# Delayed low halves, an earlier fourth split and later last-head products in a two-layer SSD and attention kernel

## The chip, the cores and the metric

The kernel runs on one core of a Trainium2 chip. The metric is the device time of one execution in microseconds, shown as the median of several runs of the same program. The engines are TensorE (PE in the profile, its weight load PEld), VectorE (DVE), ScalarE (ACT), GpSimd (POOL) and SyncE (SP), which here only starts transfers. POOL starts transfers too.

## The reference

A model of two layers at 512 positions and width 1024, in float32. Layer 0 is a state-space mixer, layer 1 is latent attention with 16 heads. Cut to the second layer, where the change lies:

```python
proj = u @ in_w
c_q, c_kv, k_r, z = split(proj)                      # 384, 256, 64, 2048 columns
q  = (rms_norm(c_q) @ uq_w)                          # 16 heads of 128 + 64 (rotated)
kv = (rms_norm(c_kv) @ ukv_w)                        # 16 heads of 128 (k) + 128 (v)
s = concat(q_nope, rope(q_rope)) @ concat(k_nope, rope(k_r)).T * scale
p = softmax(where(key <= query, s, -inf))            # causal, blocks of 128 queries
o = (p @ v).reshape(512, 2048) * silu(z)
h = h + o @ out_w
return rms_norm(h, final_norm_w)
```

## The kernel before

Every large product is made three times over in a reduced float format (fp32r): each operand is split into a high part, a cast by ACT, and a low part, the rest, a subtraction on DVE; PE then adds high x high, high x low and low x high. So each operand that reaches PE brings a cast and a subtraction, and PE has three matmuls of 128x128 by 512 where one would do.

*Weights* (`weight`, `prefetch`, `load_weight`, `split_weight`). A weight tile is 128 x 1024 (512 KB), or 128 x 640 or 128 x 512. Asking for weight i starts the load of weight i+3 from POOL's queue into one of two `raw` buffers (L303), casts weight i+2 on ACT into `whi` (L312), and puts its subtraction `wlo` (DVE, L63 of the helper) on a list. A load into a raw buffer waits until the subtraction that read the buffer is done.

*Attention.* From about 440 us the order of PE's instructions is written out by hand, and in the head loop SP, DVE, ACT and POOL also work in the written order. For head h the loop has a `feed`: the projections for later heads (`front_a`, `front_b`, `front_v` for q, k and v of a pair of heads, `zgemm` for the gate), and from head 11 on chunks of the output projection (L1061), 4, 4, 4, 8 and 10 of them. The feed yields after every six matmuls, called a tick. Between ticks stand the `pieces`, each at a share of the loop's cost:

- at SC: the four blocks of scores of head h+1 (L871, L874, L876) and then its fetch;
- at TU: `turn(h, kb)`, which splits the fetched block kb of head h: cast `ph` on ACT (L932), subtraction `pl` on DVE (L933);
- at PR: `product(h, kb)`, three matmuls with v (`po`, L947);
- at ZS = 0.8, after heads 3, 7 and 11: four silus of gates on ACT, with a change of its function table.

A score block goes through a masked minimum on DVE (L881, L883), exp on ACT (L257), a reciprocal on DVE (L889), a scaling by it (blocks 2 and 3 on ACT, L891; blocks 0 and 1 on DVE, L893) and a transpose of 32x32 tiles on DVE (`pb`, L900). Four transfers per block write it to memory (`pd<-pb`, L904), and `fetch` reads it back turned (`pl<-pd`, L925), in four transfers. Scores of a head are made one loop before its splits and products.

`defer(fn, lag)` puts an instruction off by that many ticks (`tick`), or until somebody who needs it calls `now()`. The rope of a pair's q (three DVE operations on `rraw` and `rsw`, L742 to L744) is put off by three ticks, other subtractions by one. In the output projection `out_tok` adds a chunk's result to the residual (`hr`, L1065), and `cut` makes its operands, `ah` on ACT and `al` on DVE. The output projection is made in two halves of eight heads each.

Of the kernel before, what the change touches and what calls it, by code (L numbers as in the profile page):

```python
# [10 lines left out]
F32 = mybir.dt.float32  # L11
F32R = mybir.dt.float32r
AF = mybir.ActivationFunctionType
ALU = mybir.AluOpType

P = 128
T = 512
# [6 lines left out]
MH = 16  # L24
# [17 lines left out]
G7 = 33.0  # L42
SF = (0.6, 1.0, 2.0, 3.2, 8.0)
SC = (0.0, 0.06, 0.14, 0.22, 0.6)
TU = (0.18, 0.25, 0.46, 0.57)
PR = (0.35, 0.45, 0.74, 0.94)
ZS = 0.8
KO = (4, 4, 4, 8, 10)
MID = 4
# [113 lines left out]
class Net:  # L163
# [142 lines left out]
    def split_weight(self, raw, cuts=()):  # L306
        nc = self.nc
        n = raw.shape[1]
        hi = self.whi.tile([P, n], F32R, tag="hi", name=self.nm("whi"))
        lo = self.wlo.tile([P, n], F32R, tag="lo", name=self.nm("wlo"))  # L310
        for a, b in zip((0, *cuts), (*cuts, n)):
            nc.scalar.copy(hi[:, a:b], raw[:, a:b])  # L312
            self.wlater.append(self.defer(functools.partial(
                nc.vector.tensor_tensor, lo[:, a:b], raw[:, a:b], hi[:, a:b].bitcast(F32), op=ALU.subtract)))
            yield
        yield hi, lo

# [373 lines left out]
    def mla(self):  # L691
        tc, nc, t, wk = self.tc, self.nc, self.t, self.wk
# [10 lines left out]
        for k in range(KD):  # L703
            h = self.h[k]
            a = self.act.tile([P, T], F32R, tag="ah", name=self.nm("vh"))
            b = self.act.tile([P, T], F32R, tag="al", name=self.nm("vl"))
# [6 lines left out]
        for i in range(6):  # L713
# [15 lines left out]
            while pend and i >= NU:  # L729
                o = self.o16.tile([P, T], F32, tag="o", name=self.nm("cq"))  # L730
# [16 lines left out]
        lo, hi = slice(0, 64), slice(64, 128)  # L747
# [8 lines left out]
        def zgemm(i):  # L756
            w = self.weight("w", U_MZ + i)
            ps = self.bank("mm")
            yield from self.gemm(ps[:], w, vh, vl, KD)
            z = self.o16.tile([P, T], F32, tag="o", name=self.nm("z"))  # L760
            v.tensor_tensor(z[:], ps[:], r1[:], op=ALU.mult)
            zt.append(z)
            yield 8 * 0.216
# [57 lines left out]
        def front_b(j):  # L821
            f = F[j]
            w = self.weight("ub", j)
            ps = self.bank("mm")
            yield from self.gemm(ps[:], w, qh, ql, 3)
            f["q", 1], e = qsplit(ps[:])
            f["w"].append(e)
            yield 0.2
            ps = self.bank("mm")
            yield from self.gemm(ps[:], w, kh, kl, 2, 384)  # L830
            f["k", 1], e = ksplit(ps[:])
            f["w"].append(e)
            yield 1.3

        def front_v(j):
            f = F[j]
            wh, wl = self.weight("uc", j)
            f["v"] = []
            for half in range(2):
                ps = self.bank("mm")  # L840
                for c2 in range(2):
                    c = 2 * half + c2
                    s = slice(c * P, (c + 1) * P)
                    seq = []
                    for k in range(2):
                        wc = slice(k * 256, k * 256 + 256)
                        seq += [(kh[k][:, s], wh[:, wc]), (kh[k][:, s], wl[:, wc]), (kl[k][:, s], wh[:, wc])]
                    for i, (a, b) in enumerate(seq):
                        nc.tensor.matmul(ps[:, c2 * 256:(c2 + 1) * 256], a, b, start=i == 0, stop=i == 5)
                va = wk.tile([P, T], F32R, tag="va", name=self.nm("va"), bufs=3)  # L850
                vb = wk.tile([P, T], F32R, tag="vb", name=self.nm("vb"), bufs=3)
                nc.scalar.copy(va[:], ps[:])
                f["w"].append(self.defer(functools.partial(
                    v.tensor_tensor, vb[:], ps[:], va[:].bitcast(F32), op=ALU.subtract)))
                f["v"].append((va, vb))
                yield 1.3
# [94 lines left out]
        def chain(*gs):  # L951
            for g in gs:
                yield from g
# [21 lines left out]
        def steps(h):  # L975
            return [functools.partial(score, h, b) for b in range(NCH)] + [functools.partial(fetch, h)]
# [10 lines left out]
        lo, hi = slice(0, 64), slice(64, 128)  # L987
# [11 lines left out]
        with self.tc.manual_schedule(engines={E.SP, E.DVE, E.Activation, E.Pool}):  # L999
            self.lagging, self.look = True, 2  # L1000
            self.sched(chain(front_b(0), front_v(0), zgemm(4)), list(zip(SF, steps(0))))
            for h in range(MH):
                feed, cost = [], 0.0
                j = h // 2 + 1
                if h < 14:
                    feed.append(front_a(j) if h % 2 == 0 else front_b(j))
                    cost += 5.2 if h % 2 == 0 else 5.9
                if h < 11:
                    feed.append(zgemm(5 + h))
                    cost += 5.2  # L1010
                if h >= 11:
                    k = KO[h - 11]
                    feed.append(itertools.islice(outg, k))
                    cost += 1.3 * k
                if h % 2 and h < 14:
                    feed.append(front_v(j))
                at = SC if h + 1 < MH else ()
                pieces = [(x * cost, fn) for x, fn in zip(at, steps(h + 1))]
                pieces += [(x * cost, functools.partial(turn, h, b)) for b, x in enumerate(TU)]
                pieces += [(x * cost, functools.partial(product, h, b)) for b, x in enumerate(PR)]  # L1020
                if h < 13 and h % 4 == 3:
                    pieces.append((ZS * cost, functools.partial(zsilu, h // 4 + 1)))
                if h == 10:
                    pieces.append((0.8 * cost, functools.partial(self.cut, zt, 0, 4)))
                self.sched(chain(*feed), pieces)
            self.run(outg)
            self.run(self.out_tok(zt, 1, None))

    def cut(self, o, half, n):
        done = self.cuts.setdefault(half, [])  # L1030
        while len(done) < min(n, 8):
            src = o[8 * half + len(done)][:]
            a = self.act.tile([P, T], F32R, tag="ah", name=self.nm("ah"))
            b = self.act.tile([P, T], F32R, tag="al", name=self.nm("al"))
            self.nc.scalar.copy(a[:], src)
            done.append((a, b, self.defer(functools.partial(
                self.nc.vector.tensor_tensor, b[:], src, a[:].bitcast(F32), op=ALU.subtract))))

    def out_tok(self, o, half, hd):
        nc, wk, v, t = self.nc, self.wk, self.nc.vector, self.t  # L1040
# [50 lines left out]
        for n in range(2):  # L1091
            last = half == 1 and n == 1
            cuts = [(c, 0, T) for c in range(NCH)]
            if last:
                cuts[-1:] = [(NCH - 1, 0, T // 2), (NCH - 1, T // 2, T)]
            ps = [self.bank("ot") for _ in cuts]
            base = U_OUT1 + 8 * half + 4 * n
            for u in range(2 if last else 4):
                w = self.weight("w", base + u)
                self.cut(o, half, 2 * u + 2 + OA)  # L1100
                fresh = half == 0 and u == (0 if n else 2)
                if fresh:
                    for _, _, e in hl:
                        e.now()
                for q, (c, a, b) in zip(ps, cuts):
                    if fresh:
                        r = self.o16.tile([P, T], F32, tag="o", name=self.nm("hr"))
                        nc.sync.dma_start(r[:], hd[c, :, n * T:(n + 1) * T])
                        if n == 0:
                            self.hh.append([])  # L1110
                        self.hh[c].append(r)
                    step(q, c, w, n, (2 * u, 2 * u + 1), u == 0, u == 3, a, b)
                    if b == T:
                        yield 1.3
                    if u == 3:
                        done(q, c, n)
                if half == 0 and n == 1:
                    self.cut(o, 1, 2 * u + 2)
            if last:
                w2, w3 = self.weight("w", base + 2), self.weight("w", base + 3)  # L1120
                for q, (c, a, b) in zip(ps, cuts):
                    step(q, c, w2, n, (4, 5), False, False, a, b)
                    step(q, c, w3, n, (6, 7), False, True, a, b)
                    done(q, c, n, a, b)
                    yield 2.6
# [77 lines left out]
```

## Time and profile before

| | |
|---|---|
| median of 3 runs | 855.61 us (854.59 to 856.98) |
| the profiled execution | 854.5 us |
| its span in the trace | 852.5 us |
| mean granted clock of PE | 0.991 |
| busy, share of the span | PE 96%, PEld 80%, DVE 77%, ACT 55%, POOL 6% |
| matmul records | 4068 |

Starts in the trace are counted from the span's start. The profiled execution lies 1.1 us under the median, so a time worked out in the trace is compared with 854.5 first, and then set against the median. In a row of the timeline the first two numbers are the start and the duration in us; a bracket at its end tells how long the engine had been idle and on what it waited. In a row of waits the numbers after the colon are the total, the count and the longest. `x2` at the end means two neighbours of one kind in one row.

### The profile page before, as it was taken

The numbers are of one execution on the slowest core, as the hardware profiler recorded it, in microseconds if no ns is written. First come the engines' busy times: TensorE is split into PE (matmuls) and PEld (weight loads), VectorE is DVE, ScalarE is ACT, GpSimd is POOL, SyncE is SP. The second block draws the span as 40 slices with busy tenths as digits, with TensorE's granted clock in tenths as the row PEclk, the third lists the DMA queues.
The fourth block names the chain that finished last, engine by engine and source line by source line (L and its number), as shares of the span: only waits on it lengthen the run. The fifth ranks groups of instructions, "written<-read, shape, count | busy, mean of one in ns | idle before, by whom it ended". The sixth has DMA issues, their size and how long they took to land.

```text
span 852.5 us, 11895 instructions
## 1 busy us (share of the span) xinstructions
PE 815.8 (96%) x4068; PEld 678.7 (80%) x4068; DVE 660.1 (77%) x1266; ACT 468.6 (55%) x826; POOL 50.9 (6%) x100
## 2 busy tenths in 40 slices
PE   7999999999999999999999999999999997997995
PEld 5887888888888888888888787887877876876885
DVE  6999898879888889776674978687786886865444
ACT  7566764656564648252443655556567556653233
POOL 0000000000000000000011120111101110100000
PEclk9999999999999999999999999999999999999998
DMA  7364543424242423425453256665655655576312
GB/s 224 103 193 130 168 154 99 140 84 148 92 156 75 149 88 111 136 74 148 113 139 110 64 134 160 137 142 137 158 145 138 146 156 129 138 185 175 97 63 99
DMA packets 144492, 111.57 MB, mean 131 GB/s; under 512 B 108592, under 2 KB 116272, under 8 KB 144432
## 3 DMA queue, kind: packets, MB, share of 16 engines
q1 hardware_dynamic: 134944, 79.61, 34.0%
q0 software_dynamic: 8768, 30.15, 11.7%
q10 hardware_dynamic: 720, 1.05, 0.3%
q8 instruction: 32, 0.52, 0.3%
q14 instruction: 28, 0.23, 0.1%
HBM read 93.60 MB, written 14.81 MB: 127 GB/s over the span
## 4 chain that ended last, share of the span: by engine, by line
PE 62%; DVE 13%; DMA 10%; ACT 7%; issue 4%; SPq 4%; DVEq 0%; POOL 0%; ACTq 0%
PE mm L332 40%; PE ot L1061 7%; DMA pd<-pb 4%; PE mm L341 4%; DMA pl<-pd 3%; SPq L904 3%; PE yd L149 2%; DVE wlo L63 2%; PE s L871 2%; ACT whi L312 2%; PE yd L332 1%; PE aux L141 1%; DVE pl L933 1%; PE po L947 1%; PE aux L116 1%
## 5 line engine op out<-in xcount | busy, mean ns | idle before, releaser
L312 ACT CAST whi<-raw 128x1024 fp32r<-128x1024 f32 (+3 forms) x132 | 127.0, 966 | 184.0 <-PE mm L332 162.3
L63 DVE TENSOR_TENSOR wlo<-raw,whi 128x1024 fp32r<-128x1024 f32 (+3 forms) x132 | 146.6, 1115 | 45.5 <-ACT whi L312 45.0
L332 PE MATMUL mm<-ah,whi 128*128 128x512 f32 x384 | 153.9, 401 | 0.0
L332 PE MATMUL mm<-ah,wlo 128*128 128x512 f32 x384 | 150.1, 391 | 0.4 <-DVE wlo L63 0.4
L332 PE MATMUL mm<-al,whi 128*128 128x512 f32 x384 | 149.8, 390 | 0.0
L332 PE MATMUL mm<-vh,wlo 128*128 128x512 f32 x224 | 87.7, 392 | 1.2 <-DVE wlo L63 1.2
L332 PE MATMUL mm<-vh,whi 128*128 128x512 f32 x224 | 88.3, 394 | 0.2 <-ACT whi L312 0.2
L332 PE MATMUL mm<-vl,whi 128*128 128x512 f32 x224 | 87.3, 390 | 0.0
L332 PEld LDWEIGHTS mm<-ah,wlo 128*128 128x128 f32 x384 | 72.1, 188 | 16.1 <-DVE wlo L63 0.8
L332 PEld LDWEIGHTS mm<-ah,whi 128*128 128x128 f32 x384 | 72.2, 188 | 15.4 <-issue 1.4
L332 PEld LDWEIGHTS mm<-al,whi 128*128 128x128 f32 x384 | 72.2, 188 | 14.4 <-DVE al L353 0.3
L303 POOL DMA_DIRECT2D raw<-in_w_dram x36 | 19.3, 537 | 602.4 <-DMA hd<-ht 417.0
L933 DVE TENSOR_TENSOR pl<-pl,ph 128x512 fp32r<-128x512 f32 (+1 forms) x64 | 30.8, 482 | 31.2 <-ACT ph L932 31.2
L1061 PE MATMUL ot<-whi,ah 128*128 128x512 f32 (+1 forms) x136 | 52.1, 383 | 0.0
L1061 PE MATMUL ot<-wlo,ah 128*128 128x512 f32 (+1 forms) x136 | 51.8, 381 | 0.0
L1061 PE MATMUL ot<-whi,al 128*128 128x512 f32 (+1 forms) x136 | 51.8, 381 | 0.0
L332 PEld LDWEIGHTS mm<-vh,wlo 128*128 128x128 f32 x224 | 42.0, 188 | 11.4 <-DVE wlo L63 2.1
L332 PEld LDWEIGHTS mm<-vh,whi 128*128 128x128 f32 x224 | 42.1, 188 | 8.6 <-issue 0.6
L332 PEld LDWEIGHTS mm<-vl,whi 128*128 128x128 f32 x224 | 42.1, 188 | 8.1
L257 ACT ACTIVATE p<-p,st 128x128 f32<-128x128 f32 (+1 forms) x64 | 35.6, 559 | 13.0 <-DVE st L883 12.7
L332 PE MATMUL mm<-ch,whi 128*128 128x512 f32 x104 | 42.1, 405 | 0.0
L332 PE MATMUL mm<-cl,whi 128*128 128x512 f32 x104 | 41.3, 397 | 0.0
(229 smaller groups left out, 1707.1 us busy)
## 6 DMA issues: line engine op xcount, KB each, us to landing
raw<-in_w_dram SPq DMA_DIRECT2D x64, 512.0 KB, 3.3
raw<-in_w_dram POOLq DMA_DIRECT2D x36, 512.0 KB, 3.9
L<-ac_d SPq DMA_DIRECT2D x32, 256.0 KB, 3.9
E<-ea_d SPq DMA_DIRECT2D x32, 128.0 KB, 3.6
raw<-in_ua_dram POOLq DMA_DIRECT2D x8, 512.0 KB, 4.0
pd<-pb SPq DMA_DIRECT2D x64, 64.0 KB, 2.0
pl<-pd SPq DMA_DIRECT2D x16, 256.0 KB, 2.8
pd<-pb SPq DMA_DIRECT2D x64, 48.0 KB, 1.8
```

The lines of the kernel that those rows point to most:

```text
L63: self.fn()
L116: nc.tensor.matmul(pp[c], self.BT[:, c * P:(c + 1) * P], flat(self.xw[:, c]), start=True, stop=True)
L149: nc.tensor.matmul(yd[64 * h:64 * h + 64, s], self.xdt[j][:, c, h, :], self.L[2 * j + h][:, s], start=True, stop=True)
L257: i = self.nc.scalar.activation(out, in_, func, **k)
L303: self.wqueue.dma_start(raw[:], self.t[kind][idx])
L312: nc.scalar.copy(hi[:, a:b], raw[:, a:b])
L332: self.nc.tensor.matmul(ps, a, b, start=i == 0, stop=i == len(seq) - 1)
L341: self.nc.tensor.matmul(p, seq[i][0], seq[i][1], start=i == 0, stop=i == 3 * ks - 1)
L871: nc.tensor.matmul(ps[:, :n], x[:, s], y[:, :n], start=k == 0, stop=k == 4)
L904: nc.sync.dma_start(turned[:, :n // 32, q:q + 32], pb[32 * i:32 * i + 32, :n].rearrange("a (j q) -> a j q", q=32))
L933: v.tensor_tensor(pl, pl.bitcast(F32), ph[:, :n].bitcast(F32), op=ALU.subtract)
L1061: nc.tensor.matmul(ps[:, a:b], x, y, start=start and i == 0, stop=stop and i == 5)
```

## The change

Five edits, all of order: the numbers of instructions on each engine stay as they are (the order lists 3631 on PE, 1210 on DVE, 723 on ACT, 315 on SP, 78 on POOL, before and after).

1. The subtraction `wlo` of a weight is put off by three ticks in place of one, unless the next weight is asked for earlier.
2. In TU the third split moves from 0.46 to 0.48 and the fourth from 0.57 to 0.53; PR moves from (0.35, 0.45, 0.74, 0.94) to (0.38, 0.46, 0.76, 0.95).
3. From loop 11 on the scores of the next head stand at SW, wider apart.
4. The last head has its own places for splits (TL) and products (PL), later than those of the others.
5. In the first half of the output projection, `cut` with a lag of two puts off the casts for the second half by two ticks and the subtractions by three.

```diff
-TU = (0.18, 0.25, 0.46, 0.57)
-PR = (0.35, 0.45, 0.74, 0.94)
+TU = (0.18, 0.25, 0.48, 0.53)
+PR = (0.38, 0.46, 0.76, 0.95)
+SW = (0.0, 0.1, 0.2, 0.32, 0.6)
+TL = (0.45, 0.5, 0.75, 0.82)
+PL = (0.6, 0.7, 0.88, 0.97)
...
             self.wlater.append(self.defer(functools.partial(
-                nc.vector.tensor_tensor, lo[:, a:b], raw[:, a:b], hi[:, a:b].bitcast(F32), op=ALU.subtract)))
+                nc.vector.tensor_tensor, lo[:, a:b], raw[:, a:b], hi[:, a:b].bitcast(F32), op=ALU.subtract), 3))
...
-                at = SC if h + 1 < MH else ()
+                at = (SC if h < 11 else SW) if h + 1 < MH else ()
+                last = h == MH - 1
-                pieces += [(x * cost, functools.partial(turn, h, b)) for b, x in enumerate(TU)]
-                pieces += [(x * cost, functools.partial(product, h, b)) for b, x in enumerate(PR)]
+                pieces += [(x * cost, functools.partial(turn, h, b)) for b, x in enumerate(TL if last else TU)]
+                pieces += [(x * cost, functools.partial(product, h, b)) for b, x in enumerate(PL if last else PR)]
...
-    def cut(self, o, half, n):
+    def cut(self, o, half, n, lag=0):
         done = self.cuts.setdefault(half, [])
         while len(done) < min(n, 8):
+            done.append(self.cut1(o[8 * half + len(done)][:], lag))
+
+    def cut1(self, src, lag):
...
+        def cast():
             self.nc.scalar.copy(a[:], src)
+
+        def rest():
+            first.now()
+            self.nc.vector.tensor_tensor(b[:], src, a[:].bitcast(F32), op=ALU.subtract)
+
+        first = self.defer(cast, lag)
+        if not lag:
+            first.now()
+        return a, b, self.defer(rest, lag + 1)
...
                 if half == 0 and n == 1:
-                    self.cut(o, 1, 2 * u + 2)
+                    self.cut(o, 1, 2 * u + 2, 2)
```

In the rows of order below, the number behind a name is the buffer's; line numbers of the changed kernel are 3 to 15 higher for the same code. First DVE in loop 4, behind the last transpose of head 5's scores. Splits 2 and 3 are `pl_5375` and `pl_5377`. Before:

```order
L900 STREAM_TRANSPOSE pb_5575<-p_5523 128x512
L63 TENSOR_TENSOR wlo_5566<-raw_5439,whi_5565 128x1024
L933 TENSOR_TENSOR pl_5375<-pl_5375,ph_5585 128x256
L742 TENSOR_TENSOR rraw_5472<-rraw_5472,con_3837 128x512
L743 TENSOR_TENSOR rsw_5474<-rsw_5474,con_3837 128x512
L744 TENSOR_TENSOR rraw_5472<-rraw_5472,rsw_5474 128x512
L933 TENSOR_TENSOR pl_5377<-pl_5377,ph_5597 128x128
```

Now:

```order
L903 STREAM_TRANSPOSE pb_5575<-p_5523 128x512
L936 TENSOR_TENSOR pl_5375<-pl_5375,ph_5584 128x256
L936 TENSOR_TENSOR pl_5377<-pl_5377,ph_5587 128x128
L745 TENSOR_TENSOR rraw_5471<-rraw_5471,con_3837 128x512
L746 TENSOR_TENSOR rsw_5473<-rsw_5473,con_3837 128x512
L747 TENSOR_TENSOR rraw_5471<-rraw_5471,rsw_5473 128x512
L66 TENSOR_TENSOR wlo_5566<-raw_5439,whi_5565 128x1024
```

The weight half `wlo_5566` has moved behind the rope, and both splits stand ahead of it; the other even loops look alike.

DVE at the start of loop 4, which follows the silus of loop 3, from the last v subtraction to the first reciprocal. Before:

```order
L63 TENSOR_TENSOR vb_5432<-mm_5418,va_5431 128x512
L949 TENSOR_TENSOR z_4414<-po_5330,z_4414 128x512
L63 TENSOR_TENSOR wlo_5442<-raw_5390,whi_5441 128x640
L881 TENSOR_TENSOR p_5456<-s_5452,con_3837 128x128
L883 ISA p_5456,st_5457<-s_5452,p_5456 128x128
L883 ISA st_5457 128x1
L883 ISA p_5466,st_5467<-s_5460,con_3837 128x256
L883 ISA st_5467 128x1
L883 ISA p_5487,st_5488<-s_5481,con_3837 128x384
L883 ISA st_5488 128x1
L889 RECIPROCAL st_5457<-st_5457 128x1
```

Now:

```order
L66 TENSOR_TENSOR vb_5431<-mm_5417,va_5430 128x512
L952 TENSOR_TENSOR z_4414<-po_5339,z_4414 128x512
L66 TENSOR_TENSOR wlo_5390<-raw_5315,whi_5389 128x1024
L884 TENSOR_TENSOR p_5455<-s_5451,con_3837 128x128
L886 ISA p_5455,st_5456<-s_5451,p_5455 128x128
L886 ISA st_5456 128x1
L886 ISA p_5465,st_5466<-s_5459,con_3837 128x256
L886 ISA st_5466 128x1
L886 ISA p_5486,st_5487<-s_5480,con_3837 128x384
L886 ISA st_5487 128x1
L66 TENSOR_TENSOR wlo_5442<-raw_5387,whi_5441 128x640
L892 RECIPROCAL st_5456<-st_5456 128x1
```

A 1024-wide half stands where the 640-wide one did, and that one has moved in between the third reduction and the first reciprocal. Loop 8 is alike.

Last DVE in loop 14, which splits head 14 and makes head 15's scores, from behind the first split (`hr` is the residual add, `pl_7433` split 1). Before:

```order
L883 ISA p_7550,st_7551<-s_7544,con_3837 128x512
L883 ISA st_7551 128x1
L933 TENSOR_TENSOR pl_7433<-pl_7433,ph_7553 128x384
L1065 TENSOR_TENSOR hr_7390<-ot_6950,hr_7390 128x512
L889 RECIPROCAL st_7511<-st_7511 128x1
L893 TENSOR_SCALAR p_7510<-p_7510,st_7511 128x128
L900 STREAM_TRANSPOSE pb_7565<-p_7510 128x128
L889 RECIPROCAL st_7521<-st_7521 128x1
L893 TENSOR_SCALAR p_7520<-p_7520,st_7521 128x256
L900 STREAM_TRANSPOSE pb_7573<-p_7520 128x256
L1065 TENSOR_TENSOR hr_7408<-ot_6951,hr_7408 128x512
L889 RECIPROCAL st_7539<-st_7539 128x1
```

Now:

```order
L1080 TENSOR_TENSOR hr_7384<-ot_6941,hr_7384 128x512
L66 TENSOR_TENSOR wlo_7497<-raw_7447,whi_7496 128x1024
L892 RECIPROCAL st_7510<-st_7510 128x1
L896 TENSOR_SCALAR p_7509<-p_7509,st_7510 128x128
L903 STREAM_TRANSPOSE pb_7556<-p_7509 128x128
L892 RECIPROCAL st_7520<-st_7520 128x1
L896 TENSOR_SCALAR p_7519<-p_7519,st_7520 128x256
L903 STREAM_TRANSPOSE pb_7564<-p_7519 128x256
L886 ISA p_7577,st_7578<-s_7571,con_3837 128x512
L886 ISA st_7578 128x1
L1080 TENSOR_TENSOR hr_7405<-ot_6942,hr_7405 128x512
L892 RECIPROCAL st_7541<-st_7541 128x1
```

The 512-wide reduction (`p_7550`, now `p_7577`) went from ahead of split 1 to behind block 1's transpose, and a weight half came in ahead of the first reciprocal; so the reciprocal of block 2, the last row, has that reduction and an add right ahead of it. ACT, in the same place, before:

```order
L932 CAST ph_7541<-pl_7431 128x512
L932 CAST ph_7553<-pl_7433 128x384
L257 ACTIVATE p_7538,st_7539<-p_7538,st_7539 128x384
L257 ACTIVATE p_7550,st_7551<-p_7550,st_7551 128x512
L891 ACTIVATE p_7538<-p_7538,st_7539 128x384
L891 ACTIVATE p_7550<-p_7550,st_7551 128x512
L932 CAST ph_7599<-pl_7435 128x256
```

Now:

```order
L935 CAST ph_7531<-pl_7431 128x512
L935 CAST ph_7543<-pl_7433 128x384
L260 ACTIVATE p_7540,st_7541<-p_7540,st_7541 128x384
L894 ACTIVATE p_7540<-p_7540,st_7541 128x384
L260 ACTIVATE p_7577,st_7578<-p_7577,st_7578 128x512
L935 CAST ph_7597<-pl_7435 128x256
L315 CAST whi_7607<-raw_7494 128x1024
L894 ACTIVATE p_7577<-p_7577,st_7578 128x512
```

The scaling of block 2 (`p_7540`, before `p_7538`) now stands ahead of the exponential of block 3, so that this exponential and the cast of split 2 (`ph_7597`) come behind it; the scaling of block 3 has gone behind that cast.

More of the change, by code (lines that the diff above doesn't have):

```diff
@@ L1027, in mla @@
             self.run(self.out_tok(zt, 1, None))
-    def cut(self, o, half, n):
+    def cut(self, o, half, n, lag=0):
         done = self.cuts.setdefault(half, [])
         while len(done) < min(n, 8):
-            src = o[8 * half + len(done)][:]
-            a = self.act.tile([P, T], F32R, tag="ah", name=self.nm("ah"))
-            b = self.act.tile([P, T], F32R, tag="al", name=self.nm("al"))
-            self.nc.scalar.copy(a[:], src)
-            done.append((a, b, self.defer(functools.partial(
-                self.nc.vector.tensor_tensor, b[:], src, a[:].bitcast(F32), op=ALU.subtract))))
+            done.append(self.cut1(o[8 * half + len(done)][:], lag))
+    def cut1(self, src, lag):
+        a = self.act.tile([P, T], F32R, tag="ah", name=self.nm("ah"))
+        b = self.act.tile([P, T], F32R, tag="al", name=self.nm("al"))
+        def cast():
+            self.nc.scalar.copy(a[:], src)
+        def rest():
[5 more added lines that the diff above has]
+        return a, b, self.defer(rest, lag + 1)
     def out_tok(self, o, half, hd):
```

## The prediction, made before the changed kernel ran

> **What bounds the kernel now.** I read the page's engine shares first, then the table of what TensorE (PE) waited for in three stretches, then the timeline of the head loop around each wait, then the chain of waits for the transfers.
>
> ```profile
> PE 815.8 (96%) x4068; PEld 678.7 (80%) x4068; DVE 660.1 (77%) x1266; ACT 468.6 (55%) x826; POOL 50.9 (6%) x100
> ```
>
> PE is busy 96% of an 852.5 us span and the change leaves its 4068 records alone in number and shape. So only PE's waits can be won, and time that a low granted clock costs. The change touches nothing before about 440 us, where the attention layer's manual order begins. PE's waits (total, times, longest) behind that point: the first row ends the stretch up to 500 us, the next is from 500 to 715 us (heads 0 to 11), the last two 715 to 800 us:
>
> ```profile
> PE s L874 <- DVE k L63: 0.8, 1, 0.8
> ...
> PE po L947 <- DVE pl L933: 7.8, 15, 1.5
> ...
> PE po L947 <- ACT ph L932: 6.0, 3, 3.9
> PE s L871 <- DVE vb L63: 2.9, 1, 2.9
> ```
>
> Nearly all of it is the product (L947) waiting for a split of the fetched probabilities: 7.8 us for low halves in heads 0 to 11, 6.0 us for casts in the last heads. That is what the change aims at.
>
> **Even heads: fourth split ahead of the rope, low halves of weights behind it.** Head 4, DVE then PE:
>
> ```profile
> 589.59 1.23 DVE L63 TENSOR_TENSOR wlo<-raw,whi 128x1024 fp32r<-128x1024 f32 x1
> 590.73 0.42 DVE L933 TENSOR_TENSOR pl<-pl,ph 128x256 fp32r<-128x256 f32 x1
> 593.00 0.28 DVE L933 TENSOR_TENSOR pl<-pl,ph 128x128 fp32r<-128x128 f32 x1
> ...
> 589.91 0.39 PE L947 MATMUL po<-ph,va 128*128 128x256 f32 x1
> 590.13 0.28 PE L947 MATMUL po<-ph,vb 128*128 128x256 f32 x1
> 591.21 0.38 PE L947 MATMUL po<-pl,va 128*128 128x256 f32 x1 [0.80 <-DVE pl L933]
> 592.82 0.22 PE L947 MATMUL po<-ph,va 128*128 128x128 f32 x1
> 592.88 0.27 PE L947 MATMUL po<-ph,vb 128*128 128x128 f32 x1
> 593.34 0.33 PE L947 MATMUL po<-pl,va 128*128 128x128 f32 x1 [0.19 <-DVE pl L933]
> ```
>
> Split 2 stands on DVE behind a 1.23 us weight half, split 3 behind that and three rope operations. PE's third matmul of product 2 starts 1.08 us after its second, where its first two are 0.22 apart, so 0.9 is lost; product 3 loses 0.46 less 0.06 = 0.4. In the new order both splits stand directly behind the last transpose, the weight half behind the rope. Split 2 would then end by about 590.1 (the cast before it permitting), before PE's third matmul. That is 1.3 us per even head. The delayed weight half is read only after the next chunk group, and the rope feeds scores a loop later, so I cost both moves at nothing; if that cover were gone, the 1.23 us would show as a wait of L332 on wlo. Heads 0, 2, 4, 6, 8 count; head 10's gain is lost in a later wait (below): **5 x 1.3 = -6.5**. At the start the k low half passes in front of a weight half, which takes the 0.8 wait of L874 down to about 0.2: **-0.6**.
>
> **Heads 4 and 8, after the silus.** Here the order change puts more ahead of the splits:
>
> ```profile
> 580.16 0.82 DVE L63 TENSOR_TENSOR wlo<-raw,whi 128x640 fp32r<-128x640 f32 x1
> 583.91 0.65 DVE L933 TENSOR_TENSOR pl<-pl,ph 128x512 fp32r<-128x512 f32 x1
> ...
> 583.70 0.50 PE L947 MATMUL po<-ph,va 128*128 128x512 f32 x1 [0.56 <-ACT ph L932]
> 584.62 0.50 PE L947 MATMUL po<-pl,va 128*128 128x512 f32 x1 [0.19 <-DVE pl L933]
> ```
>
> Before the first reduction now stands a 1024-wide half (1.23) in place of the 640-wide one (0.82), +0.4; the 640 one stands between the third reduction and the first reciprocal, +0.73 (0.82 less the 0.09 by which neighbours overlap, as 589.59 to 590.73 is 1.14 for a 1.23). Split 0 of the head comes 1.1 later, PE already waits there: **2 x 1.1 = +2.3**. Bounds: 0, since part of DVE's time there is waiting, and +2.3; I take the upper end, because PE's wait shows no slack.
>
> **Odd heads.** Products 0 and 1 are now back to back and six matmuls (1.36 us) later, while PE arrives 1.3 earlier:
>
> ```profile
> 601.96 0.56 DVE L933 TENSOR_TENSOR pl<-pl,ph 128x384 fp32r<-128x384 f32 x1
> 601.36 0.39 PE L947 MATMUL po<-ph,va 128*128 128x512 f32 x1
> ...
> 589.00:603.50 14.50, 13.38 (x65) 10.87 (x64) 14.20 (x32) 8.42 (x19) 1.08 (x2) 1.00 0.64 158
> ```
>
> DVE (third engine of the stretch row) is busy 14.20 of 14.50, so it gets no earlier: split 1 ends at 602.5. PE would want it at 601.36 - 1.3 + 1.36 + 0.68 (product 0) + 0.35 = 602.45. That is **5 x 0.1 = +0.5**, bounds 0 and 5 x 1.3.
>
> **The last heads.** Head 12's start, the two late waits for casts, and the granted clock (the last figures but two of the two stretch rows):
>
> ```profile
> 720.74 0.69 DVE L63 TENSOR_TENSOR vb<-mm,va 128x512 fp32r<-128x512 f32 x1 [4.71 <-ACT va L852]
> 721.49 0.80 PE L871 MATMUL s<-k,qh 128*128 128x256 f32 x2 [2.94 <-DVE vb L63]
> 764.86 0.50 PE L947 MATMUL po<-ph,va 128*128 128x512 f32 x1 [1.70 <-ACT ph L932]
> 771.12 0.39 PE L947 MATMUL po<-ph,va 128*128 128x256 f32 x1 [0.40 <-ACT ph L932]
> 784.82 0.50 PE L947 MATMUL po<-ph,va 128*128 128x512 f32 x1 [3.93 <-ACT ph L932]
> ...
> 721.50:727.70 6.20, 6.20 (x19) 5.47 (x20) 3.83 (x15) 2.73 (x9) 2.58 (x5) 0.51 0.49 138
> 784.80:788.70 3.90, 3.88 (x10) 2.77 (x11) 3.86 (x6) 2.68 (x5) 0.00 (x0) 0.61 0.93 290
> ```
>
> At 721.49 PE waits for the second half of v, whose cast stands on ACT behind the silus of loop 11. Nothing there moves, so PE coming earlier only waits longer: head 10's 1.3 and what head 11 gains end here, at cost zero, and the stretch at clock 0.51 stays. From there the scores of heads 13 to 15 are spread, and they go later:
>
> ```profile
> 733.07 0.71 DVE L900 STREAM_TRANSPOSE pb<-p 128x512 f32<-128x512 f32 x1
> 752.43 1.16 DVE L900 STREAM_TRANSPOSE pb<-p 128x384 f32<-128x384 f32 x2
> 760.89 3.23 DMA pl<-pd
> 764.84 0.69 DVE L933 TENSOR_TENSOR pl<-pl,ph 128x512 fp32r<-128x512 f32 x1 [3.62 <-ACT ph L932]
> 766.53 0.68 DVE L1065 TENSOR_TENSOR hr<-ot,hr 128x512 f32<-128x512 f32 x1
> 767.13 0.15 DVE L889 RECIPROCAL st<-st 128x1 f32<-128x1 f32 x1
> 768.79 0.65 DVE L1065 TENSOR_TENSOR hr<-ot,hr 128x512 f32<-128x512 f32 x1
> 780.57 3.51 DMA pl<-pd
> pd<-pb SPq DMA_DIRECT2D x64, 64.0 KB, 2.0
> ```
>
> The 512-wide transpose of head 14 moves from about 753.0 to 756.6 by its new place; its fetch is issued about 1 us later than 760.89, so head 14's first split X moves from 764.84 to 765.8. Behind X DVE now runs, in order: split 0 and the 384-wide reduction and split 1 (764.84 to 766.53, 1.7), the residual add (0.6, 766.53 to 767.13), a weight half (1.14), blocks 0 and 1 from reciprocal to transpose (1.66, 767.13 to 768.79), another reduction (0.6) and another add (0.6): about 6.2, and only then the reciprocal that ACT's normalise of block 2 waits for. ACT's queue is in order, and behind that normalise stand an exponential and the cast of split 2: cast ready at X + 7.9. PE wants it at X + 5.95, by the matmuls between: a new wait of 2.0 where 0.40 stood. Block 3's transpose comes at X + 11.4 (split 2, an add, block 2's transpose and the reciprocal, 1.8; the 512-wide normalise and the last cast on ACT, 1.1; split 3 and overlaps, 0.6), and the fetch 5.0 later (0.65 for the transpose, four issues at 0.5, 2.0 for the landing, 0.3); landing takes 3.5, cast and start 0.8. Head 15's first product starts at X + 20.9 = 786.7, where 784.82 stood, but by the last head's later places 12 more matmuls (2.72 us) are done before it: 1.88 - 2.72 = **-0.8**, bounds -1.5 (X unmoved) and +3 (X 767, fetch a further 2.5 late). The last wait shrinks from 3.93 to about 1.3. The stretch at 0.61 behind it loses 0.39 x 3.9 = **1.5**, which goes: waits of 1.70 brought no such stretch, 2.94 and 3.93 did.
>
> The Trainium skill ("TensorE: Matmul & The Clock Gate", Part 1: The HAM clock gate) says that the clock halves after an idle window of about 3.4 us and comes back after as long a busy one. The trace's 2.94 us already halved it, so the row decides. By the rule the new 2.0 us wait is free; a stretch like that at 784.80 behind it would make the sum 1.5 worse, 851.0.
>
> **Transfers.** Delaying a low half also delays the next load into that raw buffer, from POOL's queue, which has to wait for it:
>
> ```profile
> 609.25 0.53 POOL L303 DMA_DIRECT2D raw<-in_w_dram  x1 [4.76 <-DVE wlo L63]
> 610.90 4.12 DMA pd<-pb
> 615.09 2.96 DMA pl<-pd
> ```
>
> With that load in flight a write of 64 KB landed in 4.12 against a median of 2.0. The load moves to 612 to 613, into the read; the writes leave 0.85 earlier, since reciprocals no longer stand behind it. I take **+0.5** over heads 2, 6, 10, bounds -2 and the third rival. The deferred casts of the output chunk (lag 2) are read some 80 matmuls later; the rope's swaps on POOL come about 1 us later behind a load, and the rope was not waiting: nothing, with a wait of L1061 on al or of L742 as the sign that it was something.
>
> **Sum.** -6.5 - 0.6 + 2.3 + 0.5 - 0.8 - 1.5 + 0.5 = -6.1. The profiled run took 854.5, 1.1 under the median of 855.6; set against the median: **849.5**.
>
> **Rivals.** *(1) The late waits vanish:* if head 14's fetch keeps its time, the 3.93, the 1.5 of clock and the 1.70 go together, -7.1 in place of -2.3: 844.7. For it: 12 more matmuls of cover; against it the six DVE operations counted above. *(2) The gain is handed back:* PE arrives 1.3 earlier at the odd heads, DVE does not, and PE waits there. Odd heads then cost 5 x 1.3 in place of 0.5, the rest being as in the sum: 855.5. For it: DVE's 14.20 of 14.50; against it the 1.36 by which the products move, which covers exactly this. *(3) Slower:* the moved weight loads run beside the fetches. With a landing late by d, heads 2, 6, 10 lose d + 0.4, five odd heads what exceeds 1.5, the last three d - 1, d and d, and the clock's 1.5 returns. At d = 1.3 that is 5.1 + 0.3 + 2.6 + 1.5 - 0.5 = 9.0, 858.5; at d = 2.1, the 4.12 less 2.0, 866. It decides from d = 1.3. For it: that one row; against it, only a load that starts within the fetch's 3 us meets it. The Trainium skill ("DMA: Bandwidth & Descriptors", Issuing engines are not separate DMA queues) says that transfers started by different engines interleave on the same 16 DMA engines; the 4.12 agrees, and that rule speaks for this rival. *(4)* That the order does not change is excluded: the rows of both orders differ.
>
> **Chances.** Forecast (846 to 853) 0.50, late waits vanish 0.14, handed back 0.21, slower 0.15. A difference under 0.3% (2.6 us) can hardly be told from none; so faster 0.64, same 0.21, slower 0.15. The range takes the first two and the handed-back case up to 856.5, leaving out rival 3 and a little at each end: 843.0 to 856.5.
>
> **What would show it.** Right: in 500 to 715 us the 7.8 for low halves falls to about 3, with the 1.08 gap at product 2 of even heads gone; split 0 of heads 4 and 8 waits about 1.1 longer; head 12 still starts behind vb with a wait over 4; a wait of about 2 in the middle of head 14; the last head waits 1 to 2 and no stretch at 0.61 follows. Wrong: odd heads wait 1 us each (rival 2), landings of 3 us and more in even heads' fetches (rival 3), or waits of L332 on wlo.

## Result: slower by 1%, and the profile after

The changed kernel takes 864.21 us (median of 4, 863.17 to 865.20) against 855.10 us for the kernel before (median of 4, 853.72 to 856.98). The ratio is 1.0105 (95% interval 1.0081 to 1.0129). The prediction was 849.5 us, faster; the time lies outside its range, and in the price range of its third rival (858 to 866).

The profiled execution took 863.17 us, span 861.4 us, 8.9 us over the span before. Engine shares of the page, to be held against the row shown before:

```profile
PE 818.2 (95%) x4068; PEld 681.5 (79%) x4068; DVE 660.3 (77%) x1266; ACT 468.0 (54%) x826; POOL 50.6 (6%) x100
```

All engines have the same counts, and DVE and ACT the same busy time to 0.6 us. PE is busy 2.4 us longer at a mean clock of 0.986 (0.991 before); the rest is waiting. PE's waits, again up to 500 us, then 500 to 715 us, then 715 to 800 us:

```profile
PE s L877 <- DVE k L66: 0.2, 1, 0.2
...
PE po L950 <- ACT ph L935: 10.7, 7, 4.2
PE s L879 <- DVE s L816: 3.8, 4, 1.0
PE po L950 <- DVE pl L936: 1.8, 2, 0.9
...
PE s L874 <- DVE vb L66: 4.5, 1, 4.5
PE po L950 <- ACT ph L935: 4.5, 3, 1.8
PE po L950 <- DVE pl L936: 0.5, 1, 0.5
```

The waits for the low halves `pl` are indeed nearly gone (7.8 to 1.8 us). In their place stand 10.7 us for the casts `ph`, where 2.0 stood, and a wait that was not there at all: the scores (L879) wait 3.8 us for the low halves of the rope's result (L816).

How far each head's end (the product's multiplication with the gate, one DVE row per head) lies behind the same row of before, in us, worked out from the starts of those rows:

| end of head | 1 | 3 | 5 | 7 | 9 | 11 | 13 | 15 |
|---|---|---|---|---|---|---|---|---|
| changed kernel | 3.7 | 4.9 | 6.7 | 6.9 | 8.3 | 10.7 | 11.4 | 8.9 |

So the loss is made in the loop ahead of head 0 and in head 0 (3.7), and then by each even loop up to loop 10; odd loops up to head 9 give 0.2 to 0.8 back. Heads 13 to 15 together win 1.8 (10.7 to 8.9): heads 13 and 14 lose another 2.7, and head 15 wins 4.5.

**Where an even loop loses.** Loop 2, before, POOL's transfers:

```profile
539.12 0.53 POOL L303 DMA_DIRECT2D raw<-in_w_dram  x1 [5.04 <-DVE wlo L63]
543.97 2.04 POOL L738 DMA_DIRECT2D rsw<-rraw  x4 [4.33 <-ACT rraw L790]
```

And after, with DVE's transpose and PE's product behind them:

```profile
546.99 0.53 POOL L306 DMA_DIRECT2D raw<-in_w_dram  x1 [3.98 <-DVE st L886]
547.64 1.99 POOL L741 DMA_DIRECT2D rsw<-rraw  x4
...
556.37 0.58 DVE L903 STREAM_TRANSPOSE pb<-p 128x384 f32<-128x384 f32 x1 [3.45 <-DMA pd<-pb]
...
559.04 0.39 PE L950 MATMUL po<-ph,va 128*128 128x256 f32 x1 [1.55 <-ACT ph L935]
```

The last part of the fetch there, in the chain of the changed kernel (start, duration to the landing):

```profile
547.60 6.94 DMA pl<-pd
```

The weight load of 512 KB left 4.9 us ahead of the rope's swaps; now it leaves 0.65 us ahead of them, and with the fetch. That part of the fetch lands after 6.94 us; its size, 64 KB, had a median of 4.5 before. (The bracket of the load at 546.99 names the reduction that DVE ended last by then; the subtraction that frees the raw buffer ended half a microsecond ahead of it, at 546.45.) The writes of block 0 land so late that the transpose of block 2 has no buffer to go to: there are two `pb` tiles, and block 2 takes that of block 0. DVE stands 3.45 us, with all that is queued behind it: the transpose, ACT's scalings that wait for DVE's reciprocals, and ACT's casts of splits 2 and 3 in the queue behind those. PE then waits for the cast, 1.55 us, and the 4 us behind that run at a granted clock of 0.63 (the last figure but two), where before the 4 us from that product on had 1.00:

```profile
559.00:563.00 4.00, 3.96 (x13) 3.26 (x14) 3.95 (x7) 1.53 (x4) 0.00 (x0) 0.63 0.49 84
```

By 0.37 of 4 us that is another 1.5 us, as an estimate, about as much as the wait. Over 495 to 715 us, DVE's wait for a buffer, before:

```profile
DVE pb L900 <- DMA pd<-pb: 3.8, 5, 1.7
```

and after:

```profile
DVE pb L903 <- DMA pd<-pb: 12.5, 6, 3.7
```

And the median landing of the rope's swaps in that stretch (the last number), before:

```profile
rsw<-rraw POOLq DMA_DIRECT2D x24, 64.0 KB, 2.4
```

and after:

```profile
rsw<-rraw POOLq DMA_DIRECT2D x24, 64.0 KB, 4.8
```

### The profile page after: what moved, and what is told of

Its sections match the earlier page's. It is cut to its first block, busy times and chain, and to the rows that moved or that the text cites. A ratio compares the mean times of both kernels' runs of the same rounds, so it can differ in the third digit from the quotient of the medians.

```text
span 861.4 us, 11890 instructions
## 1 busy us (share of the span) xinstructions
PE 818.2 (95%) x4068; PEld 681.5 (79%) x4068; DVE 660.3 (77%) x1266; ACT 468.0 (54%) x826; POOL 50.6 (6%) x100
## 4 chain that ended last, share of the span: by engine, by line
PE 68%; DVE 13%; DMA 8%; ACT 6%; issue 3%; SPq 2%; POOL 0%; DVEq 0%; ACTq 0%
PE mm L335 44%; PE ot L1076 6%; PE mm L344 4%; DMA pd<-pb 3%; PE s L874 3%; DVE wlo L66 2%; PE po L950 2%; DMA pl<-pd 2%; PE yd L152 2%; PE mm L852 2%; ACT whi L315 1%; PE yd L335 1%; PE aux L144 1%; PE aux L119 1%; DMA x<-in_x_dram 1%
## 5 line engine op out<-in xcount | busy, mean ns | idle before, releaser
L335 PE MATMUL mm<-ah,whi 128*128 128x512 f32 x384 | 153.8, 401 | 0.0
L335 PE MATMUL mm<-ah,wlo 128*128 128x512 f32 x384 | 150.1, 391 | 0.4 <-DVE wlo L66 0.4
L335 PE MATMUL mm<-al,whi 128*128 128x512 f32 x384 | 149.8, 390 | 0.0
L335 PE MATMUL mm<-vh,wlo 128*128 128x512 f32 x224 | 88.6, 396 | 1.2 <-DVE wlo L66 1.2
L335 PE MATMUL mm<-vh,whi 128*128 128x512 f32 x224 | 89.2, 398 | 0.5 <-ACT whi L315 0.5
L335 PE MATMUL mm<-vl,whi 128*128 128x512 f32 x224 | 88.4, 395 | 0.0
L335 PEld LDWEIGHTS mm<-ah,wlo 128*128 128x128 f32 x384 | 72.1, 188 | 16.1 <-DVE wlo L66 0.8
L335 PEld LDWEIGHTS mm<-ah,whi 128*128 128x128 f32 x384 | 72.2, 188 | 15.4 <-issue 1.4
L335 PEld LDWEIGHTS mm<-al,whi 128*128 128x128 f32 x384 | 72.2, 188 | 14.4 <-DVE al L356 0.3
L335 PEld LDWEIGHTS mm<-vh,wlo 128*128 128x128 f32 x224 | 42.7, 191 | 11.5 <-DVE wlo L66 2.1
L335 PEld LDWEIGHTS mm<-vh,whi 128*128 128x128 f32 x224 | 42.7, 191 | 9.2 <-ACT whi L315 0.7
L335 PEld LDWEIGHTS mm<-vl,whi 128*128 128x128 f32 x224 | 42.7, 190 | 8.2
L903 DVE STREAM_TRANSPOSE pb<-p 128x128 f32<-128x128 f32 (+1 forms) x64 | 32.3, 509 | 18.3 <-DMA pd<-pb 12.5
L335 PE MATMUL mm<-ch,whi 128*128 128x512 f32 x104 | 42.4, 407 | 0.0
```

The source lines that it names most:

```text
L335: self.nc.tensor.matmul(ps, a, b, start=i == 0, stop=i == len(seq) - 1)
L903: v.transpose(pb[:, :n], p[:])
```

## The experiments

A profile is one execution; single executions of one kernel here lie up to 0.6% on either side of their median. So the conclusions go by the medians and ratios, and a profile tells where time goes in its execution. Runs 1 to 4, 5 to 8, 9 to 11, and 12 come from four chips, each with the kernel before measured beside them (854.0 to 854.9 us); a ratio is to that.

Two theories stood against each other. *A, late loads:* the late low half frees its raw buffer late, the next load bunches with other transfers, and DVE and ACT wait for landings. *B, places:* the new places of splits, products and halves cost by themselves.

### 1. The low halves at one tick again, all else as changed

```diff
-    ... hi[:, a:b].bitcast(F32), op=ALU.subtract), 3))
+    ... hi[:, a:b].bitcast(F32), op=ALU.subtract)))
```

> The changed kernel with the weights' low halves one tick behind their casts again, all else kept. Theory A (late loads): a low half three ticks late frees its raw buffer late, the next weight load then runs beside the swaps and the score writes, and casts and transposes wait for transfers; so undoing this alone takes away the +10.6 us that loops 0 to 10 gained, and the late heads' -1.7 stays: 852 to 854 us, and DVE waits for pd<-pb between 495 and 715 us for no more than 5 us (12.5 now). Theory B (the places of splits and products, or the order on DVE without transfers, cost it): 860 us or more, with product 2 of even heads still waiting for its cast.

Measured 854.1 us, ratio 0.9998 (0.9974 to 1.0022) to before, at the edge of what theory A said. DVE's wait for a buffer is back at what it was:

```profile
DVE pb L903 <- DMA pd<-pb: 3.6, 4, 1.5
```

Some ten microseconds hang on the lag alone; the other four edits together are worth nothing measurable.

### 2. The late halves alone, in the kernel before

> The kernel before with the low halves three ticks late and nothing else. Theory A: nearly the whole loss, 863 to 866 us. Theory B: 854 to 857 us.

Measured 865.14 us, ratio 1.0130 (1.0091 to 1.0169). The lag is enough by itself. With run 1, theory B falls as far as it meant the places of splits and products.

### 3. The changed kernel with more buffers for the transposes

```diff
-                pb = wk.tile([P, T], F32, tag="pb", name=self.nm("pb"))
+                pb = self.res.tile([P, T], F32, tag="res", name=self.nm("pb"))
```

The score tiles' pool has eight buffers, of which a head used four; no instruction moves.

> The changed kernel with the transposed tiles pb taken from the pool of the score tiles (eight buffers) instead of two of their own; the order of every engine is the same. If the writes that land late reach PE by the transposes that wait for a free pb, DVE's waits for pd<-pb (12.5 us) go to about 0 and 5 to 8 us come back: 856 to 859 us. If they reach it by the fetches, or the late casts of weights on ACT (11.2 us of waits for loads) set the pace: 862 us or more.

Measured 853.82 us, ratio 0.9990 (0.9967 to 1.0013): as much as the loss is back, more than expected (run 7 tells how much of it was the change's own). The transposes' waits for `pd<-pb` are gone from DVE's table; 0.5 us, of a split, are left. The swaps still land slowly (5.1 us, median), and ACT still waits for late loads (6.2 us over 495 to 715 us, 11.2 before this edit); but PE's waits in 500 to 715 us fall to

```profile
PE po L950 <- ACT ph L935: 4.9, 3, 3.7
PE po L950 <- DVE pl L936: 2.4, 3, 1.0
PE s L879 <- DVE s L816: 1.8, 2, 0.9
```

So the bunched transfers reach PE through the two buffers of the transposes. In this profile head 2 wins 1.4 us against before and head 6 also 1.4, near the 1.3 that the prediction gave to an even head; part of that is the pool's, for against the kernel before with the same pool (run 7) each wins 0.9. Heads 4 and 8 lose 1.1 and 1.5.

### 4. A third raw buffer as well

> As the run before, and a third raw buffer for weights, so that a load need not wait for the late low half (the first layer's loads move a little too). Theory A: loads start as early as in the kernel before, ACT's waits for loads are gone, and the earlier splits show: 847 to 853 us. Theory B: no better than the run before it.

Measured 856.38 us, ratio 1.0020 (0.9996 to 1.0045): a miss for theory A, and what theory B said. What theory A said of the waits came: ACT waits for no load, and head 0's product no longer waits 3.70. But the third buffer also moves loads in the first layer, where PE waits 4.2 us at once for a weight half (up to 500 us it waits 5.2 for weight halves, 1.6 before), and head 0 still ends 4.0 us late. From head 1 to head 9 this profile gains 1.1 us and run 3's 2.6, so ACT's waits for loads were not what held run 3 back there. The time settles nothing between the theories, since the edit reaches outside the head loop.

### 5. and 6. One half in six

In each pair of heads there is one low half, of the 1024-wide weight ahead of the 640-wide one, which three ticks carry past both v halves into the next loop, since v's loop ticks only twice in 24 matmuls. Its raw buffer is what the load of loop 2's 546.99 waited for. Run 5 puts these seven halves back in the changed kernel, run 6 moves only these in the kernel before.

```diff
+            k, n = self.wq[self.wpos][0], (self.wq + [("", 0)])[self.wpos + 1][0]
-            w = list(self.split_weight(self.wraws.pop(0)))[-1]
+            w = list(self.split_weight(self.wraws.pop(0), lag=1 if (k, n) == ("w", "ub") else 3))[-1]
```

> The changed kernel with one low half in each pair of heads put back to one tick: that of the 1024-wide weight ahead of the 640-wide one, which the changed order puts behind both v halves and whose raw buffer the next load waits for. Theory A (that load runs into fetch, swaps and writes): 853 to 856 us, and DVE waits for pd<-pb at most 5 us. Rival (the late halves cost by their places on DVE, all of them, or the casts on ACT wait for every late load): 859 us or more.

> The kernel before with only these halves (7 in all) three ticks late. Theory A: most of the loss by itself, 860 to 865 us. Rival: 854 to 857 us.

Run 5: 857.27 us, ratio 1.0033 (1.0011 to 1.0054), DVE's wait for buffers 6.6 us; between both expectations (its buffer waits are above theory A's 5). The profiled execution is the slowest of ten, 3.8 us over the median. The load of loop 2 leaves 3.4 us ahead of the swaps there. Its head 1 ends 3.8 us late, like the changed kernel's, but from there to head 9 it loses nothing (3.3 at head 9, where the changed kernel is at 8.3). Run 6: 861.76 us, ratio 1.0090 (1.0057 to 1.0122), as theory A said; the load of loop 2 leaves 0.6 us ahead of the swaps, and the profile is 0.8 us late at head 1, 6.8 at head 9:

```profile
DVE pb L901 <- DMA pd<-pb: 11.5, 5, 3.8
```

So these seven halves are enough for a loss as large as that of the even loops, and the changed kernel without them does not make it. The match is not loop by loop: in run 6 loop 2 itself wins 0.9 us, and loops 4, 6 and 8 lose. The first 3.7 us are another matter: in the loop ahead of head 0 all halves at three ticks delay a load by 4.3 us (POOL issues it at 494.81, before at 490.54), and ACT, in order, stands before the cast of that weight. The cast, and then head 0's first product, of the changed kernel, and in a fence of its own the 4 us behind that:

```profile
498.47 1.05 ACT L315 CAST whi<-raw 128x1024 fp32r<-128x1024 f32 x1 [2.75 <-DMA raw<-in_ua_dram]
...
516.61 0.79 PE L950 MATMUL po<-ph,va 128*128 128x512 f32 x1 [4.16 <-ACT ph L935]
```

```profile
516.60:520.60 4.00, 3.99 (x9) 3.10 (x10) 3.42 (x9) 2.93 (x7) 0.00 (x0) 0.50 0.25 41
```

Scores, writes and fetch of head 0 are late by it, PE waits 4.16 (0.87 before) and runs the 4 us behind it at clock 0.50 (last row), half of which is lost.

### 7. The kernel before with the pool for transposes

> The kernel before with pb from the pool of the score tiles. It had 3.8 us of DVE waits for pd<-pb behind 495 us: if they were on the path, 851 to 853 us; if, as its PE waits say, the splits' places set the pace, 853.5 to 855 us. Then the changed kernel with the same pool (853.8) is no better than this.

Measured 850.26 us, ratio 0.9956 (0.9934 to 0.9977), better than expected. The kernel before already paid for its two buffers. With the pool in both kernels the change still costs some 3 us (2.9 by the ratios of runs 3 and 7, 3.6 by their medians, which come from two chips), and with two buffers it costs 9. So about 6 us go by the buffers, and something else of the change costs the other 3. The delay at head 0 is still there in run 3 (head 1 ends 2.9 us late, 0.7 in run 7) and would be of that size; but the two profiled executions have the same span, 849.2 us, so the profiles can't show that it is this.

### 8. The repairs together

The changed kernel with the pool, the one half at one tick, and one tick in the loop ahead of head 0.

> The changed kernel with pb from the pool of the score tiles, the one half back to one tick, and all halves at one tick in the loop ahead of head 0. Theory A: even loops 2, 6, 10 keep -1.3 each, loops 4 and 8 no longer lose 1.1 and 1.5, loop 0 loses no 3: 845 to 849 us. Rival (the gains are swallowed by the wait for v at head 12): 850 us or more.

Measured 853.03 us, ratio 0.9990 (0.9967 to 1.0013): a miss for theory A, in the rival's range. Head 0's wait is 0.56 in place of 3.70 (run 3) and no buffer is waited for. But at head 12 PE waits 4.13 us for v, where the kernel before has 2.94. PE's table for 500 to 715 us is led by

```profile
PE s L881 <- DVE s L818: 5.3, 6, 1.0
```

once per even loop. In loop 4 of this run, DVE between the last splits and the rope's low halves, and PE:

```profile
589.42 0.63 DVE L938 TENSOR_TENSOR pl<-pl,ph 128x256 fp32r<-128x256 f32 x2 [0.53 <-ACT ph L937]
589.97 0.68 DVE L747 TENSOR_TENSOR rraw<-rraw,con 128x512 f32<-128x512 f32 x1
...
591.89 1.22 DVE L66 TENSOR_TENSOR wlo<-raw,whi 128x1024 fp32r<-128x1024 f32 x1
593.03 0.69 DVE L766 TENSOR_TENSOR z<-mm,rr 128x512 f32<-128x512 f32 x1
593.75 0.68 DVE L818 TENSOR_TENSOR s<-rraw,s 64x512 fp32r<-64x512 f32 x1
...
594.49 0.39 PE L881 MATMUL s<-k,s 128*128 128x256 f32 x1 [0.94 <-DVE s L818]
```

The rope's result is needed by the first score of the next loop, 3 us later, not a loop later. The weight half that went behind the rope (591.89) stands ahead of the low half of its result, 1.14 us of it, and PE, which arrives earlier, waits 0.94.

### 9. That half behind the rope's low halves

The same with a lag of six for the weight ahead of the v weight, which puts it behind both rows of L818.

> The mix of the run before (the one half at one tick, pb from the score pool), with the half that stood between the rope and the low halves of its results put behind these. Theory C (the early splits' gain is handed back in even loops, where the next head's first score waits about 0.94 us for the low halves of the rope, a weight half being ahead of them): these waits go and 847 to 850 us. If the score would have waited for something else at that place: 852 us or more.

Measured 852.88 us, ratio 0.9979 (0.9963 to 0.9996). The waits for the rope are gone from PE's table, and head 9 ends 2.5 us ahead of before (1.0 in run 8). But 1.2 of this 1.5 was there at the end of head 1. From there to head 9, where four waits for the rope (3.5 us) went, run 9 gains 2.8 us and run 8 gained 2.5: waits for splits, 2.6 us in place of 1.4, took up a part of it. So the wait was taken away as expected, and most of its time did not come back. At the end of head 11 run 9 is 0.2 ahead: it loses the rest by a wait of 1.40 for head 10's first split (none there before) and by 4.12 for v at head 12 (2.94 before).

### 10. The last head's places alone

The kernel before with the pool and TL and PL, no other edit.

> The kernel before with pb from the score pool (850.3) and the last head's later places TL and PL, without the spread scores. If cover is all that the last head lacked, its wait of 3.6 us shrinks by 2.7 and the stretch at clock 0.61 behind it goes: 845.5 to 848 us. If the splits or the transfers of the last head are late anyhow: 849 to 851 us.

Measured 847.84 us (846.76 to 848.78), ratio 0.9920 (0.9903 to 0.9937), as expected, the fastest of all, and better than both kernels. Before head 15 the wait is 1.00 us where run 7 has 3.62, and the 3.9 us behind it have clock 1.00, where run 7 has 0.60:

```profile
781.30 0.50 PE L950 MATMUL po<-ph,va 128*128 128x512 f32 x1 [1.00 <-ACT ph L935]
```

```profile
781.30:785.20 3.90, 3.90 (x16) 3.00 (x17) 1.61 (x3) 0.96 (x3) 0.00 (x0) 1.00 0.75 267
```

Against the kernel before, head 15 wins 4.35 us in this profile: the wait, 3.93 there, is 2.9 shorter, and the clock, 0.61 there, makes 1.5. The profile also has luck in it: the wait of 2.93 for v at head 12 is followed by clock 1.00, the same wait in run 7 by 0.57.

### 11. The parts from head 11 on alone, in the kernel before

> The kernel before with the parts from head 11 on alone (spread scores, last head's places, deferred casts of the output chunk). The prediction's terms for them, -0.8 and -1.5: 851 to 853 us, heads 13 and 14 each ending later and head 15 earlier. If they were worth nothing: 854 to 855.5 us.

Measured 853.0 us, ratio 0.9975 (0.9957 to 0.9993), at the edge of what the prediction's terms gave. Heads 13 and 14 together lose 2.8 us against before, and head 15 wins 3.4. In run 10, without the spread scores and the deferred casts, heads 13 and 14 lose nothing. So in the profiles these two pay most of what the last head's places earn; by the medians, 2.4 us of run 10 over run 7 against 1.6 here over before, the difference is too small to tell.

### 12. All that proved good

Run 9 without the spread scores and the deferred casts.

> All that proved good at once: the changed places TU and PR, pb from the score pool, the halves as in the run with the half behind the rests, the last head's later places, and the old places of the scores (no spread, no deferred casts). Against the last-head-only kernel (847.8) it differs in the early heads' part alone, which was 2 us ahead by head 9. If that reaches the end: 845 to 846.5 us. If it is swallowed between heads 10 and 12, by the wait for v behind the silus: 847.5 to 849.5 us.

Measured 854.03 us, ratio 0.9994 (0.9971 to 1.0018), 850.57 to 858.01: worse than both expectations. Its profile is its fastest execution and shows the swallowing: 3.2 us ahead of before at head 9, 0.35 at head 11, with these waits on the way (the kernel before has none at the first place, 1.52 at the second and 2.94 at the third); behind the second 4 us run at clock 0.69:

```profile
687.03 0.50 PE L952 MATMUL po<-ph,va 128*128 128x512 f32 x1 [1.35 <-ACT ph L937]
707.04 0.50 PE L952 MATMUL po<-pl,va 128*128 128x512 f32 x1 [2.12 <-DVE pl L938]
721.13 0.51 PE L876 MATMUL s<-k,qh 128*128 128x256 f32 x2 [2.94 <-DVE vb L66]
```

PE comes early to heads 10 and 11, and their first splits do not. Why this kernel's median is 6 us over run 10's, when the profiled executions differ by 3.8, the one profile can't say; that stays open, as does which of the bunched transfers delays the writes most.

## Why the prediction was wrong, step by step

- *Even heads, -6.5.* The size for one head was near where it could show (1.4 in heads 2 and 6 of run 3 against before, 0.9 against run 7). Two covers were named at no cost, and both failed. "The delayed weight half is read only after the next chunk group": true of PE (no wait of L335 on wlo there), but the half also frees the raw buffer. "The rope feeds scores a loop later": the next loop's first score comes 3 us later, and with a weight half ahead of the rope's low halves PE waits 0.94 there in most even loops (run 8); moving that half away gave little of it back (run 9). Nor does the sum of the heads reach the end: leads of 2.5 and 3.2 us at head 9 (runs 9 and 12) are 0.2 and 0.35 at the end of head 11.
- *Transfers, +0.5.* This is the step that failed by most. The prediction saw the load move and quoted a write at 4.12 us, but took a small toll for it, and looked for the damage at the fetch. It missed that two `pb` buffers couple a late write to DVE's order: 12.5 us of waits. The lag costs 10 us or more (runs 1 and 2), and about 6 of the loss go by these buffers (runs 3 and 7), where the term had 0.5. It also missed the loop ahead of head 0 and the clock behind the new waits. Some 3 us of the loss stay with the pool; that loop (head 1 ends 3.7 us late, 2.9 with the pool) would fill them, but run 8, which repairs it too, is no faster than run 3, so they stay open. Rival 3 named the cause, moved loads, and had the time inside its prices, at a chance of 0.15; that the price fitted is in part luck, for its path, splits that wait for late fetches, was not the main one.
- *Start, -0.6.* Right: L877 waits 0.2 for the k half.
- *Heads 4 and 8, +1.1 each.* Right in kind: run 3 shows split 0 there waiting 0.97 in place of 0.19, and the heads 1.1 and 1.5 behind.
- *Odd heads, +0.1 each.* Right: no wait for splits in heads 1 to 9; the handed-back gain (rival 2) did come, but in the even loops, by the rope.
- *Head 12.* The wait came, 4.5 us for v where over 4 was expected, but not for the reason given, that nothing ahead of v's cast moves. Before, ACT waits for PE ahead of that cast, and v comes earlier when PE does: run 7 reaches head 12 1.4 us earlier, with the same wait of 2.94. In the changed kernel ACT waits there for DVE's reciprocal of block 3, which stands behind a weight half. The first row is of the kernel before, the others of the changed one:

```profile
713.05 1.05 ACT L312 CAST whi<-raw 128x1024 fp32r<-128x1024 f32 x1 [0.98 <-PE ot L1061]
...
722.36 1.18 DVE L66 TENSOR_TENSOR wlo<-raw,whi 128x1024 fp32r<-128x1024 f32 x1
723.46 0.15 DVE L892 RECIPROCAL st<-st 128x1 f32<-128x1 f32 x1
723.71 0.72 ACT L894 ACTIVATE p<-p,st 128x512 f32<-128x512 f32 x1 [2.22 <-DVE st L892]
```

  The same wait of 2.22 is there in runs 3, 8 and 9 and not in run 12, which has the old places of the scores. In run 12 the gains are swallowed from head 10 on.
- *Last heads, -0.8 and -1.5.* Right nearly to size: the new wait in head 14 is 1.8 (2.0 expected), the last head's 1.4 (1.3), the stretch at 0.61 behind that is gone, and heads 13 to 15 win 1.8. (The steps to head 15's first product add up to X + 20.7, not 20.9, so the term would have been -1.0.) Run 11 has 1.6 us for these parts alone. Their rows, and the 4 us behind each:

```profile
784.24 0.39 PE L950 MATMUL po<-ph,va 128*128 128x256 f32 x1 [1.77 <-ACT ph L935]
797.98 0.50 PE L950 MATMUL po<-ph,va 128*128 128x512 f32 x1 [1.37 <-ACT ph L935]
```

```profile
784.20:788.20 4.00, 3.96 (x13) 3.15 (x14) 2.94 (x7) 3.09 (x5) 0.00 (x0) 0.64 0.60 122
798.00:802.00 4.00, 4.00 (x17) 3.09 (x18) 3.93 (x6) 1.86 (x4) 0.00 (x0) 1.00 0.85 284
```

A stretch at 0.64 now follows the wait of 1.77 in head 14 instead, the case priced at 1.5 (851.0). The Trainium skill ("DMA: Bandwidth & Descriptors", Issuing engines are not separate DMA queues) was the rule that spoke against the change: transfers of SP and POOL share the engines. The 6.94 us of the fetch from SP's queue, with POOL's load and swaps under way, agree with it; the swaps' 2.4 to 4.8 us can't tell, since the load ahead of them is in POOL's own queue.

## What to carry to other kernels

When an operation is put off, ask what its end frees, not only who reads its result: here a subtraction off the critical path set when a load began, the late load came together with other transfers, and writes that landed late held buffers that DVE, in its written order, needed. Before moving work, count the buffers behind each transfer that may land later; going from two to a shared pool gave 0.4% without moving one instruction. "Needed a loop later" is worth a look at the first instruction of that loop.

## What the runs showed of the hardware

The granted clock did not follow the length of a wait alone. In the 4 us behind it (each figure is their mean), 1.55 us in loop 2 of the changed kernel brought 0.63. In head 14, waits of 1.77 us (changed kernel) and 1.75 us (run 3) brought 0.64 and 0.67, the same wait of 1.77 in run 8 and of 1.73 in run 9 brought 1.00. At other places 2.93 in run 10 and 3.18 in run 12 brought 1.00, and 2.72 in run 11 brought 0.59. The prediction's reading, that 1.70 is safe and 2.94 is not, came from one execution and does not hold. The Trainium skill ("TensorE: Matmul & The Clock Gate", Part 1: The HAM clock gate) speaks of an activity window that runs freely; that a like wait is or is not followed by a lower clock agrees, but a lower clock behind 1.55 us is well under its idle window of about 3.4.
